# A decoder layer on one core: the two ends of SBUF swapped

## The chip, the cores and the metric

The kernel runs on one core of a Trainium2 chip. A run's time is the device time of that core in microseconds (us); before the change it is 2342.14 us, the median of three runs (2342.01 to 2342.49). Durations inside the kernel are read from one profiled execution.

## What is computed

One layer of a decoder for 256 tokens of width 2048, in float32: a SwiGLU block, a mixer of four branches, a second SwiGLU block, each followed by a residual and a layer norm.

```python
h <- LN(alpha*h + 0.5*SwiGLU_1(h))          # [256, 2048] @ [2048, 11264], then [256, 5632] @ [5632, 2048]
h <- LN(alpha*h + HybridMixer(h))           # projection, 4 causal mixers, 4 gates, 4 branch products, w_out
h <- LN(alpha*h + 0.5*SwiGLU_2(h))

def swiglu(h, w_gu, w_down):
    gate, up = jnp.split(h @ w_gu, 2, axis=-1)
    return (jax.nn.silu(gate) * up) @ w_down

# the end of the mixer: outs are the results of differential attention, GLA, MLA and SSD
merged = gates[:, :, 0] * (outs[0] @ w_branch[0])
for i in range(1, 4):
    merged = merged + gates[:, :, i] * (outs[i] @ w_branch[i])
return merged @ w_out
```

## The kernel before

**Products.** Every large product is token-major. The transposed activation (128 x 128) is the stationary operand, a weight tile (128 x 512) the moving one. A float32 product is made of three float32r ones: each operand is split exactly into a high and a low part, and `mm3` (lines 130 to 133) accumulates high x high (L131), high activation x low weight (L132) and low activation x high weight (L133). There are 9,510 such products with 512 moving columns, 192 with 300 (the narrow blocks `pm` of the input projection) and 66 with 256 (in the MLA mixer). All other products, transposes against `ident` among them, are plain float32 ones of at most 512 columns.

**The way of a weight.** `load_split` loads a group of 1 MB by DMA (SyncE's queue) into one of three buffers `raw`; `split` makes of each half of it, a chunk of 1024 columns, a tile `hi` (ScalarE, L99) and a tile `lo` (VectorE, L100); TensorE reads `hi` and `lo` as moving operands. `split` takes its tiles from two pools in turn:

```python
if self.hl2 is not None and k % 10 >= 4:
    p, b = self.hl2, 6
else:
    p, b = self.hl, 4
```

So of ten chunks the first four go to the pool `hl` and the next six to `hl2`, as long as `hl2` is open: through the first SwiGLU and the first three blocks of the projection (as `hla`), and from the output projection `wo` to the end (as `hlb`). In between, from the rest of the projection through the gates `gt` and the branch products `br`, all weights use `hl` alone, and the space of `hl2` is the mixers'.

**Order.** Each engine takes its instructions in the order in which the program writes them. The mixers' steps are put between groups of the streamed products by hand (`tick`, `MIX_STEPS`), TensorE's queue is one row of products from start to end.

**Places in SBUF.** A pool is opened at one end of SBUF, `side="left"` (low addresses, the default) or `side="right"` (high addresses), and lies against the pools opened before it at that end. A partition has 224 KB; the low end begins after 16.125 KB that are taken, the high end 32 bytes below 224 KB. All sizes in the pools of TensorE's operands at issue are whole multiples of 512 bytes or more, so what a pool starts at, counted in 64 bytes, decides for all of its tiles. The addresses in the built program (KB of a partition; the last column is the remainder of the byte address by 64):

| what | before | by 64 | after | by 64 |
|---|---|---|---|---|
| `xp`: activations, high and low part (stationary) | 18.75 to 50.75 | 0 | 16.125 to 48.125 | 0 |
| `raw`: loaded weights | 50.75 to 74.75 | 0 | 197.34 to 221.34 | 32 |
| `hl`: `hi`, then `lo` (moving) | 74.75 to 106.75 | 0 | 48.125 to 80.125 | 0 |
| `hl2`: `hi`, then `lo` (moving) | 175.97 to 223.97 | 32 | 80.125 to 128.125 | 0 |
| `oh`, `ol`: branch outputs, split (stationary in `br`) | 186.22 to 194.22 | 32 | 80.125 to 88.125 | 0 |
| `cqh`, `cql`, `ckh`, `ckl`: MLA's inner operands | 175.5 to 183.5 | 0 | 88.125 to 96.125 | 0 |
| `ident`: identity for transposes (moving) | 16.125 | 0 | 221.34 | 32 |
| `ya`: rows of the first SwiGLU (stationary in transposes) | 106.75 to 122.75 | 0 | 180.97 to 196.97 | 32 |
| `mg`: merged branches (stationary in transposes) | 158.22 to 174.22 | 32 | 129.88 to 145.88 | 0 |
| `bg`: gate biases (DMA target) | 174.22 to 178.22 | 32 | 117.88 to 121.88 | 0 |

Before, `xp` and `hl` start at multiples of 256 bytes; after, all rows with remainder 0 start at odd multiples of 128.

The functions that the change touches, with the profile's line numbers:

Of the kernel before, what the change touches and what calls it, by code (L numbers as in the profile page):

```python
"""Macaron decoder layer (SwiGLU, hybrid differential / GLA / MLA / SSD mixer, SwiGLU; post-norm).

Activations are token-major: the transposed activation is the stationary operand and each weight is
streamed once from DRAM as the moving operand. float32 products are made of float32r ones: both
operands are split exactly into two parts of 12 significant bits, and the three products that reach
float32's accuracy are accumulated in PSUM.
"""
# [9 lines left out]
F32R = mybir.dt.float32r  # L17
# [18 lines left out]
# columns of the array of constants  # L36
C_ID, C_MLE, C_MGT, C_CM, C_CUM, C_SUF, C_GM, C_IND, C_INV = 0, 128, 256, 384, 640, 768, 896, 1024, 1026
C_END = 1026 + 40
# columns of the array of parameters that are broadcast over the partitions
R_LAM, R_SUB, R_GN, R_SN, R_D, R_DTB, R_AL, R_GB, R_QN, R_KN = 0, 256, 384, 512, 1024, 1032, 1040, 1048, 1304, 1688  # L40
R_END = 1816
# blocks of the input projection
# [3 lines left out]
# steps of the mixers that go between two groups of a streamed product  # L46
MIX_STEPS = 3
# after how many runs of products a norm's parts are transposed, by token tile and part
WAIT = ((3, 4, 5, 6), (4, 5, 6, 7))
# products on zeros that bring TensorE's clock up  # L50
# [3 lines left out]
def two_pi_parts(scale, bits, n):  # L54
    """2*pi*scale as a sum of n floats: the first n-1 with so many significant bits."""
# [15 lines left out]
class Layer:  # L71
# [9 lines left out]
    def pool(self, name, side="left", bufs=1, **kw):  # L81
        return self.tc.tile_pool(name=name, bufs=bufs, side=side, reuse_waits="tile", **kw)

# [1 line left out]

    def split(self, src, n, name, step=None):
        """Exact two-part split of an f32 source into float32r tiles."""
# [15 lines left out]
    def load_split(self, w, name, fine=False):  # L103
        """One weight group [128, nk, n] -> list of (hi, lo) per k tile."""
# [30 lines left out]
    def gemm(self, name, ws, x, evac, lag=0, tail=0, pre=None, parts=None, ahead=None):  # L135
        """Token-major product: ws are weight groups [128, nk, n]; x(g, k, t) gives the stationary
        tiles; evac(t, psum) takes the result of token tile t. The second token tile follows the first
        by `lag` groups at the start, and by `tail` groups at the end. parts: groups that are loaded
        already; ahead(t): called before token tile 0 is evacuated and after token tile 1 is."""
# [38 lines left out]
    def loader(self, name, ws):  # L178
        """ahead() for the block before the one that is named: its weights are loaded and split
        before the norm in between takes the engines."""  # L180
        parts = {}

        def ahead(t):
            for g in (range(2), range(2, 3))[t]:
                parts[g] = self.load_split(ws[g], f"{name}_{g}", fine=t)

        return parts, ahead

# [30 lines left out]
    def transpose_split(self, src, name):  # L219
        """[128 tokens, 512] -> [128 of a feature tile, (4 feature tiles, 128 tokens)] in a bank."""  # L220
# [11 lines left out]
    def rstd(self, pool, ms, n, eps, name, scale=None):  # L232
        """(ms + eps) ** -0.5 for [128, n]."""
# [15 lines left out]
    def layer_norm(self, name, pool, y, stats, t, xs=None, store=None):  # L249
        """Post-norm of token tile t (in place in y); then its transposed parts, or its store."""  # L250
# [5 lines left out]
        # the first parts of the first token tile are waited for: VectorE; the others are shared out  # L256
# [12 lines left out]
        for nb in range(4):  # L269
# [6 lines left out]
            if xs is not None:  # L276
                # not before they can be ready: after so many runs of products
# [86 lines left out]
    def residual(self, y, stats, t, nb, ps):  # L364
        """y = 2 alpha h + what was accumulated, and its statistics."""
# [93 lines left out]
    def to_banks(self, pool, tag, blocks, name, bufs=3, eng=0):  # L459
        """Transposes of up to four [128, 128] blocks into one bank; copied to SBUF."""  # L460
# [12 lines left out]
    def o_room(self):  # L473
        """Lets the branch products take an earlier mixer's output first."""
        while self.o_live > 4:
            yield "full"

    def head_norm(self, pool, o, r, g, t, name):
        """o[:, h, :] * r[:, h] * g, per head of 128."""
# [18 lines left out]

    def mla(self, m):
        nc, gp = self.nc, self.gen  # L500
        with self.pool("mla", side="right") as w:
# [37 lines left out]
            # rope of the key  # L539
            cm, sm = self.cos[:, :, 8:40], self.sin[:, :, 8:40]  # L540
            yield from self.rope(w, kv[:, :, 128:160], kv[:, :, 160:192], cm, sm, [P, T, 32], "rk")
            # for even and odd heads: in one half of the rows, zeros in the other
# [6 lines left out]
            # up-projections: heads' parts without rotation come out transposed  # L549
# [127 lines left out]

    def diff(self, blk):
        nc, gp = self.nc, self.gen
        with self.pool("diff", side="right") as w:  # L680
# [7 lines left out]
            # -(lambda) = (e2 - lam_init) - e1  # L688
# [24 lines left out]
            for t in range(T):  # L713
# [5 lines left out]
                for h0 in range(0, 4, nm):  # L719
                    # the maps of a head in different rows of the array and in different banks  # L720
# [52 lines left out]

    def gla(self, blk, sm):
        nc, gp = self.nc, self.gen
        row = self.row
        with self.pool("gla", side="right") as w:
            qk, v, rr = blk[B_GQK], blk[B_GV], blk[B_GR]
            with self.pool("glaa", side="right") as wa:
# [24 lines left out]
                # sums within a chunk: up to each token, and after it  # L804
# [16 lines left out]
                # decay of the state over each chunk, per channel  # L821
# [23 lines left out]
            # states that enter chunks 1, 2, 3  # L845
# [25 lines left out]
            with self.pool("glab", side="right") as wb:  # L871
                # silu(r), twice
# [656 lines left out]
```

## Time and profile before

| | |
|---|---|
| median of three runs | 2342.14 us |
| span of the profiled execution | 2340.0 us |
| TensorE, products | 2316.7 us, 99% of the span, 10,433 instructions |
| TensorE, loads of stationary operands (beside products) | 1888.4 us, 81% |
| VectorE | 1334.5 us, 57% |
| ScalarE | 1091.1 us, 47% |
| GpSimd | 106.0 us, 5% |
| DMA | 446 MB, 191 GB/s, 55.3% of 16 engines' time |

The span runs from the first to the last instruction of the profiled execution; the median of the timed runs is 2.1 us more. Products are pipelined: one begins some 0.23 us after the one before it and is shown as 0.39 us long, so that a busy share of 99% says that TensorE hardly waits, not how fast its products follow each other. That is read from their starts, or from a count in a stretch that holds products of one kind alone.

### The profile page before, as it was taken

Reading aid. Unit: us, or ns where it says so; the run is one execution under the profiler, and the core shown is the slowest. Engines: PE = TensorE matmul, PEld = TensorE weight load, DVE = VectorE, ACT = ScalarE, POOL = GpSimd, SP = SyncE. Lnnn points to the kernel's source line nnn. Section 1 sums busy time; section 2 is a strip of 40 time slices with the busy share of each in tenths; the row PEclk is TensorE's granted clock in tenths of the full one; section 3 lists DMA queues with packets and bytes.
Section 4 is the critical chain, followed back from the end, with each engine's and each line's share of the span. In section 5 each row is a group of like instructions: output and inputs, shape, how many; then the busy total and the mean of one; then the engine's idle time right before and its main releaser. Section 6 shows DMA issues by size and latency. Waiting matters only on the chain.

```text
span 2340.0 us, 26513 instructions
## 1 busy us (share of the span) xinstructions
PE 2316.7 (99%) x10433; PEld 1888.4 (81%) x10433; DVE 1334.5 (57%) x1523; ACT 1091.1 (47%) x1400; POOL 106.0 (5%) x107
## 2 busy tenths in 40 slices
PE   9999999999999999999999999999999999999998
PEld 7888888888887988787788888887888888888886
DVE  6544444457676457646655555756444444457674
ACT  5444444455554445545444444534444444455552
POOL 0000000000001100100001011112000000000001
PEclk9999999999999999999999999999999999999999
DMA  8655555555564555454455557645555555555562
GB/s 320 221 182 192 183 181 193 184 182 195 186 228 162 176 196 171 137 191 172 167 189 201 199 198 267 233 160 191 187 182 192 183 182 193 183 183 195 185 228 72
DMA packets 73165, 446.05 MB, mean 191 GB/s; under 512 B 8513, under 2 KB 8913, under 8 KB 22865
## 3 DMA queue, kind: packets, MB, share of 16 engines
q1 hardware_dynamic: 73040, 444.37, 55.3%
q8 instruction: 81, 1.33, 0.2%
q14 instruction: 44, 0.35, 0.0%
HBM read 440.15 MB, written 4.19 MB: 190 GB/s over the span
## 4 chain that ended last, share of the span: by engine, by line
PE 97%; DVE 1%; POOL 0%; ACT 0%; issue 0%; DMA 0%; POOLq 0%; SPq 0%; DVEq 0%; ACTq 0%
PE f_gu_ps L132 14%; PE f_gu_ps L133 14%; PE f_gu_ps L131 14%; PE f_dn_ps L131 7%; PE f_dn_ps L132 7%; PE f_dn_ps L133 7%; PE gt_ps L131 5%; PE gt_ps L133 5%; PE gt_ps L132 5%; PE pj_ps L133 3%; PE pj_ps L132 3%; PE pj_ps L131 3%; PE br_ps L131 1%; PE br_ps L133 1%; PE br_ps L132 1%; PE wo_ps L131 1%
## 5 line engine op out<-in xcount | busy, mean ns | idle before, releaser
L100 DVE TENSOR_TENSOR f_gu_lo<-f_gu_raw,f_gu_hi 128x1024 fp32r<-128x1024 f32 (+1 forms) x362 | 434.6, 1207 | 435.0 <-ACT f_gu_hi L99 425.2
L99 ACT CAST f_gu_hi<-f_gu_raw 128x1024 fp32r<-128x1024 f32 (+1 forms) x362 | 370.1, 1027 | 451.5 <-PE f_gu_ps L133 415.3
L131 PE MATMUL f_gu_ps<-f_gu_hi,n_x_h 128*128 128x512 f32 x704 | 281.5, 400 | 0.4 <-ACT n_x_h L229 0.4
L131 PE MATMUL f_gu_ps<-f_gu_hi,x_h 128*128 128x512 f32 x704 | 280.9, 399 | 0.6 <-ACT f_gu_hi L99 0.6
L133 PE MATMUL f_gu_ps<-f_gu_hi,n_x_l 128*128 128x512 f32 x704 | 277.4, 394 | 3.3 <-DVE n_x_l L230 3.3
L132 PE MATMUL f_gu_ps<-f_gu_lo,x_h 128*128 128x512 f32 x704 | 277.0, 394 | 0.5 <-DVE f_gu_lo L100 0.5
L132 PE MATMUL f_gu_ps<-f_gu_lo,n_x_h 128*128 128x512 f32 x704 | 277.4, 394 | 0.0
L131 PE MATMUL f_dn_ps<-f_dn_hi,f_a_h 128*128 128x512 f32 x704 | 277.2, 394 | 0.0
L132 PE MATMUL f_dn_ps<-f_dn_lo,f_a_h 128*128 128x512 f32 x704 | 276.8, 393 | 0.0
L133 PE MATMUL f_dn_ps<-f_dn_hi,f_a_l 128*128 128x512 f32 x704 | 276.6, 393 | 0.0
L133 PE MATMUL f_gu_ps<-f_gu_hi,x_l 128*128 128x512 f32 x704 | 276.4, 393 | 0.0
L100 DVE TENSOR_TENSOR f_dn_lo<-f_dn_raw,f_dn_hi 128x1024 fp32r<-128x1024 f32 x176 | 215.0, 1222 | 35.2 <-ACT f_dn_hi L99 34.7
L100 DVE TENSOR_TENSOR gt_lo<-gt_raw,gt_hi 128x1024 fp32r<-128x1024 f32 x128 | 156.8, 1228 | 134.6 <-ACT gt_hi L99 130.1
L336 ACT CAST f_a_h<-f_act 128x512 fp32r<-128x512 f32 x176 | 108.8, 618 | 209.8 <-PE f_dn_ps L132 200.0
L99 ACT CAST gt_hi<-gt_raw 128x1024 fp32r<-128x1024 f32 x128 | 134.6, 1053 | 149.9 <-PE gt_ps L133 107.4
L131 PE MATMUL gt_ps<-gt_hi,n_x_h 128*128 128x512 f32 x512 | 200.0, 391 | 0.0
L132 PE MATMUL gt_ps<-gt_lo,n_x_h 128*128 128x512 f32 x512 | 199.4, 389 | 0.0
L133 PE MATMUL gt_ps<-gt_hi,n_x_l 128*128 128x512 f32 x512 | 199.4, 389 | 0.0
L337 DVE TENSOR_TENSOR f_a_l<-f_act,f_a_h 128x512 fp32r<-128x512 f32 x176 | 121.2, 689 | 120.0 <-ACT f_a_h L336 120.0
L99 ACT CAST f_dn_hi<-f_dn_raw 128x1024 fp32r<-128x1024 f32 x176 | 184.5, 1048 | 9.8 <-PE f_gu_ps L133 9.8
L133 PEld LDWEIGHTS f_gu_ps<-f_gu_hi,n_x_l 128*128 128x128 f32 x704 | 132.7, 188 | 34.2 <-DVE n_x_l L230 3.8
L132 PEld LDWEIGHTS f_gu_ps<-f_gu_lo,x_h 128*128 128x128 f32 x704 | 132.5, 188 | 30.1 <-DVE f_gu_lo L100 1.8
(366 smaller groups left out, 3390.2 us busy)
## 6 DMA issues: line engine op xcount, KB each, us to landing
f_gu_raw<-in_wgu SPq DMA_DIRECT2D x172, 1024.0 KB, 4.8
f_dn_raw<-in_wdn SPq DMA_DIRECT2D x88, 1024.0 KB, 4.9
gt_raw<-in_wg SPq DMA_DIRECT2D x64, 1024.0 KB, 4.9
pj_raw<-in_wp SPq DMA_DIRECT2D x36, 1024.0 KB, 4.8
br_raw<-in_wb SPq DMA_DIRECT2D x16, 1024.0 KB, 4.8
wo_raw<-in_wo SPq DMA_DIRECT2D x16, 1024.0 KB, 4.8
pm_raw<-in_wm SPq DMA_DIRECT2D x8, 600.0 KB, 4.3
f_gu_raw<-in_wgu SPq DMA_DIRECT2D x16, 256.0 KB, 5.5
```

The costliest lines, as they stand in the source:

```text
L99: nc.scalar.copy(hi[:, c], src[:, c])
L100: nc.vector.tensor_tensor(lo[:, c], src[:, c], hi[:, c].bitcast(F32), op=ALU.subtract)
L131: nc.tensor.matmul(ps, xh, wh, start=start, stop=False)
L132: nc.tensor.matmul(ps, xh, wl, start=False, stop=False)
L133: nc.tensor.matmul(ps, xl, wh, start=False, stop=stop)
L336: nc.scalar.copy(hi, src)
L337: nc.vector.tensor_tensor(lo, src, hi.bitcast(F32), op=ALU.subtract)
```

## The change

`pool()` opens pools at the high end unless told otherwise, and the pools that held a side explicitly change it. With that, `xp`, `hl`, `hl2` and the mixers' own pools (`mla`, `diff`, `gla`, `ssd` and their inner ones) lie at the low end; constants and `ident` (`cp`), `raw`, the rows of activations, the mixer's constants and outputs at the high end. `oh` and `ol` leave the pool of the gates for a new one, `mxl`, which is opened at the low end when `hla` is closed. Comments and docstrings are removed as well. The diff without those:

```diff
-    def pool(self, name, side="left", bufs=1, **kw):
+    def pool(self, name, side="right", bufs=1, **kw):
...
-        with self.pool("mla", side="right") as w:
+        with self.pool("mla", side="left") as w:
...   (diff, gla, glaa, glab, ssd, ssda, ssdb in the same way)
             self.hl2 = None
             hl_pool.close()
+            ml = st.enter_context(self.pool("mxl", side="left"))
...
-                    hi = mp.tile([P, 512], F32R, tag="oh", bufs=2, name=f"oh{i}_{t}")
-                    lo = mp.tile([P, 512], F32R, tag="ol", bufs=2, name=f"ol{i}_{t}")
+                    hi = ml.tile([P, 512], F32R, tag="oh", bufs=2, name=f"oh{i}_{t}")
+                    lo = ml.tile([P, 512], F32R, tag="ol", bufs=2, name=f"ol{i}_{t}")
...
-        self.xp = ent(self.pool("xp"))
+        self.xp = ent(self.pool("xp", side="left"))
         self.rawp = ent(self.pool("rawp"))
-        self.hl = ent(self.pool("hl"))
+        self.hl = ent(self.pool("hl", side="left"))
...
-            self.hl2 = st.enter_context(self.pool(name, side="right"))
+            self.hl2 = st.enter_context(self.pool(name, side="left"))
```

No instruction is added, removed or moved: on every engine the built program has the same instructions in the same order. What differs beside addresses is which semaphores an instruction waits for where a tile takes over another tile's place: in 8 instructions of VectorE, 31 of ScalarE, 16 of GpSimd and 15 DMA issues of SyncE, and in none of TensorE. The tables of addresses above are the change.

## Rows read from the trace of the kernel before

**Rows 1.** The page, parts 1 and 2: busy time; the granted clock in 40 slices.

```profile
PE 2316.7 (99%) x10433; PEld 1888.4 (81%) x10433; DVE 1334.5 (57%) x1523; ACT 1091.1 (47%) x1400; POOL 106.0 (5%) x107
PEclk9999999999999999999999999999999999999999
```

**Rows 2.** The page, part 4: the chain that ended last, shares by engine.

```profile
PE 97%; DVE 1%; POOL 0%; ACT 0%; issue 0%; DMA 0%; POOLq 0%; SPq 0%; DVEq 0%; ACTq 0%
```

**Rows 3.** Waits of TensorE: line, releaser, us in total, times, longest; the longest three.

```profile
PE f_gu_ps L133 <- DVE n_x_l L230: 3.3, 1, 3.3
PE pj_ps L133 <- DVE n_x_l L230: 3.3, 1, 3.3
PE diff_q L704 <- DVE pj L442: 1.6, 1, 1.6
```

**Rows 4.** Stretches of TensorE: from:to, us, PE busy (count), clock, DMA share, GB/s.

```profile
1264.73:1308.02 43.29, 43.29 (x192) 1.00 0.57 200
1253.54:1264.50 10.96, 10.96 (x48) 1.00 0.60 198
510.47:745.76 235.29, 235.29 (x1022) 1.00 0.56 193
780.30:806.75 26.45, 26.45 (x192) 1.00 0.68 227
4.90:32.60 27.70, 26.61 (x108) 1.00 0.88 320
```

**Rows 5.** TensorE in order of time, in `f_gu`: start us, us, line, operands.

```profile
299.69 0.39 PE L131 MATMUL f_gu_ps<-f_gu_hi,x_h 128*128 128x512 f32 x1
...
301.05 0.40 PE L131 MATMUL f_gu_ps<-f_gu_hi,x_h 128*128 128x512 f32 x1
301.28 0.40 PE L132 MATMUL f_gu_ps<-f_gu_lo,x_h 128*128 128x512 f32 x1
...
303.15 0.40 PE L131 MATMUL f_gu_ps<-f_gu_hi,x_h 128*128 128x512 f32 x1
```

**Rows 6.** The same view, in the MLA mixer: `ckh`, `ckl` stationary.

```profile
849.74 0.39 PE L131 MATMUL mla_v<-ukv_hi,ckh 128*128 128x512 f32 x1
849.96 0.39 PE L132 MATMUL mla_v<-ukv_lo,ckh 128*128 128x512 f32 x1
850.19 0.39 PE L133 MATMUL mla_v<-ukv_hi,ckl 128*128 128x512 f32 x1
850.42 0.39 PE L131 MATMUL pj_ps<-pj_hi,n_x_h 128*128 128x512 f32 x1
```

**Rows 7.** The same view, 256 columns: second and last of 54 in a row.

```profile
830.19 0.28 PE L132 MATMUL mla_q<-cql,uq_hi 128*128 128x256 f32 x1
...
836.43 0.28 PE L133 MATMUL mla_qr<-uq_hi,cql 128*128 128x256 f32 x1
```

**Rows 8.** Groups by line: transposes against `ident`; count, busy us, mean ns, idle before.

```profile
L224 PE MATMUL n_tp<-ident,ya 128*128 128x128 f32 x32 | 4.8, 272 | 0.0
L224 PE MATMUL mT_tp<-ident,mg 128*128 128x128 f32 x32 | 4.1, 272 | 0.0
```

**Rows 9.** The page, parts 5, 3 and 6: splits; DMA queue; DMA issues, KB, us to landing.

```profile
L100 DVE TENSOR_TENSOR f_gu_lo<-f_gu_raw,f_gu_hi 128x1024 fp32r<-128x1024 f32 (+1 forms) x362 | 434.6, 1207 | 435.0 <-ACT f_gu_hi L99 425.2
L100 DVE TENSOR_TENSOR gt_lo<-gt_raw,gt_hi 128x1024 fp32r<-128x1024 f32 x128 | 156.8, 1228 | 134.6 <-ACT gt_hi L99 130.1
q1 hardware_dynamic: 73040, 444.37, 55.3%
f_gu_raw<-in_wgu SPq DMA_DIRECT2D x172, 1024.0 KB, 4.8
bg<-in_b_gate SPq DMA_DIRECT2D x16, 256.0 KB, 3.4
f_gb<-in_ln_g SPq DMA_DIRECT2D x8, 256.0 KB, 3.4
```

More of the change, by code (lines that the diff above doesn't have):

```diff
@@ L679, in diff @@
         nc, gp = self.nc, self.gen
-        with self.pool("diff", side="right") as w:
+        with self.pool("diff", side="left") as w:
             row = self.row
@@ L776, in gla @@
         row = self.row
-        with self.pool("gla", side="right") as w:
+        with self.pool("gla", side="left") as w:
             qk, v, rr = blk[B_GQK], blk[B_GV], blk[B_GR]
-            with self.pool("glaa", side="right") as wa:
+            with self.pool("glaa", side="left") as wa:
                 w2 = wa.tile([16, 256], F32, name="gla_w2")
@@ L870, in gla @@
                 yield
-            with self.pool("glab", side="right") as wb:
+            with self.pool("glab", side="left") as wb:
                 sr = wb.tile([P, T, 512], F32, name="gla_sr")
@@ L950, in ssd @@
         row = self.row
-        with self.pool("ssd", side="right") as w:
+        with self.pool("ssd", side="left") as w:
             x = w.tile([P, T, 8], F32, name="dt_x")
@@ L982, in ssd @@
             yield
-            with self.pool("ssda", side="right") as wa:
+            with self.pool("ssda", side="left") as wa:
                 xc = [(wa if j < 2 else w).tile([P, 2, 256], F32, name=f"ssd_xc{j}") for j in range(4)]
@@ L1023, in ssd @@
                 yield
-            with self.pool("ssdb", side="right") as wb:
+            with self.pool("ssdb", side="left") as wb:
                 BT, CT = xc[2], xc[3]
```

## The prediction

> **What bounds the kernel now.** I read the page's busy times first, then the chain, then TensorE's waits, then stretches of TensorE with one kind of product each, and last single products in order of time. TensorE is busy for 99% of the span, at a granted clock of nine tenths or more in all forty slices, which is the upper of its two levels, 2.4 GHz [rows 1]; 97% of the chain that ended last is TensorE's own work [rows 2]; and the longest waits in its list are 3.3, 3.3 and 1.6 us [rows 3]. So there is almost nothing to wait for. What can be won is how fast one product follows another, and this the busy share hides, since a product is shown as 0.39 us long while the next one begins after 0.23 us.
>
> So I count starts. In the gates `gt` 192 products with 512 columns take 43.29 us from the first start to the last, which is 191 steps of 226.6 ns. In the branch products `br`, whose instruction is the same, 48 take 10.96 us: 47 steps of 233.2 ns. In `f_dn` some 1,020 steps take 235.29 us: 230.7 ns. [rows 4] (A count may hold a product or two that run in from ahead.) Weights come from `hl` alone in `gt` and `br`. In `f_dn` they come from `hl` for four chunks of ten and from `hl2` for six, and 0.4 x 226.6 + 0.6 x 233.2 = 230.6, which is what is seen if products on `hl2` take the step of `br`. The single products show that it is so: in one block of `f_gu` six products on an `hl` chunk take 301.05 - 299.69 = 1.36 us, 226.7 ns each, and the nine that follow, on `hl2` chunks with the same kind of stationary operand, take 303.15 - 301.05 = 2.10 us, 233.3 ns each [rows 5]. The step changes at the product where the chunk's pool changes. At 2.4 GHz, 226.7 ns are 544 cycles and 233.3 ns are 560: the slow step is 16 cycles longer.
>
> What slow products have in common is one operand at the high end: `hl2` tiles (moving) or `oh`, `ol` (stationary, in `br`). These lie both high, above 175 KB, and at a remainder of 32 bytes by 64, because the high end begins 32 bytes below 224 KB. The trace has a few products that separate the two. The last three products of `mla_v` have stationary operands at 182 and 183 KB, high but at remainder 0: they start at 849.74, 849.96, 850.19 and the next at 850.42, three steps of 226.7 ns [rows 6]. With 256 columns, 36 of 54 products have moving operands at 175.5 to 183.5 KB, remainder 0, the other 18 stationary ones there: 52 steps in 6.24 us, 120.0 ns [rows 7], which is 256 cycles and the same 32 on top as the fast step. So the condition is more likely the remainder than the height. The 300-column products in `pm` step at 26.45 us / 191 = 138.5 ns [rows 4], 300 cycles and 32, on both pools alike; they start 1200 bytes apart inside a chunk, at several remainders, and do not separate the two.
>
> **The change part by part.**
>
> *Moving operands.* 4,056 products with 512 columns read a weight from `hl2` in the built program: 2,520 in `f_gu`, 1,248 in `f_dn`, 216 in `wo`, 72 in `pj`. After the change `hl2` lies low and at remainder 0. Each should step at 226.7 instead of 233.3 ns: 4,056 x 6.67 ns = 27.0 us.
>
> *Stationary operands.* 384 products of `br` get `oh` and `ol` at the low end, remainder 0: 384 x 6.67 ns = 2.6 us. Together 29.6 us, all of it on TensorE, which is the chain.
>
> *Where the gain is not on the path.* From 4.9 to 32.6 us, 108 products take 27.70 us, 259 ns a step, since the first weights are still coming (320 GB/s) [rows 4]; some 59 of them read `hl2`, so up to 59 x 6.67 = 0.4 us is not won. I take off the 0.4.
>
> *`ident` moves to the high end at remainder 32.* Some 400 plain float32 transposes with 128 columns read it as moving operand. The trace has none with a moving operand at that remainder. The nearest rows are those where the stationary side is at it (`mg`, remainder 32) and where it isn't (`ya`): both 272 ns [rows 8]. From this I take 0. The upper end is the step of the float32r products for each, 400 x 6.67 = 2.7 us; a gain is excluded, since `ident` lay at remainder 0 already.
>
> *`raw` moves to remainder 32.* VectorE's split takes 1,207 ns in `f_gu`, where six of ten destinations are at remainder 32, and 1,228 ns in `gt`, where none is [rows 9]; no row has the source there. VectorE at 57% and ScalarE at 47% [rows 1] have room for a third more, so I take 0 with no end that reaches the path. For the DMA, 256 KB to `bg` (remainder 32) land in 3.4 us and 256 KB to `f_gb` (remainder 0) in 3.4 us [rows 9]: 0. A group of weights is needed every 24 x 226.7 ns = 5.4 us and lands 4.8 us after its issue with three buffers, while the queue is busy for 55.3% of 16 engines' time [rows 9]; it would have to become 1.8 times as slow before TensorE waits.
>
> A rule speaks against this move. The Trainium skill, DMA: Bandwidth & Descriptors, section "How a descriptor splits into AXI transactions", says that a descriptor which does not start on 256 bytes spends an extra transaction; `raw` starts on such a boundary before and not after. By that page, a row of 8 KB would be 33 transactions instead of 32, an estimated 3% more, so 55.3% would become about 57%, and the sum would stay the same.
>
> *Waits.* No wait of TensorE changes in the program. The changed ones on other engines stand where pools change hands, ahead of the mixers and of `hlb`; those engines run ahead of TensorE by up to ten chunks there. 0, with 1 us as the upper end, the size of the third of the longest waits now [rows 3].
>
> Sum: the span goes from 2340.0 to 2340.0 - 29.6 + 0.4 = 2310.8 us. The median of the runs is 2.1 us above the span, and I carry that over: 2342.1 - 29.2 = **2312.9 us**, 1.2% faster. The unknowns reach from -0.4 (the start gains too) to +2.7 + 1.0, so 2312.5 to 2316.6 by themselves; for the steps, which are read to about 0.2 ns over 9,500 products, I add 2 us on either side.
>
> **The rivals.**
>
> *The edge is lower than all slow rows.* If height decides, the edge lies anywhere between 107 KB (fast) and 176 KB (slow). At 112 KB, the middle of the partition, the four upper `lo` tiles of `hl2` (112.1 to 128.1 KB) would stay slow: 900 products of L132, 6.0 us. Time 2318.9. [rows 6] speak against height at all.
>
> *Nothing changes.* The slow step would come from the turn in the ring, or from what else runs while `hl2` is read, not from the place: 2342.1. Against it: `br` has the slow step with weights from `hl`, and it begins and ends with the operand [rows 4]. For it: only that the trace never shows a low operand at remainder 32. By a statement of the Trainium skill (SBUF — State Buffer, "Door 1", on cachelines) SBUF has lines of 16 bytes, and an access pays where it crosses to a new line; by that, addresses at remainder 32 are as good as those at 0, and this rival's time would follow. The trace disagrees where `br` takes 233.2 ns and `gt` 226.6.
>
> *Slower: the grid is 256 bytes.* All fast 512-column products of before have operands at multiples of 256. After the change every operand is at an odd multiple of 128. If a product needs 256, all 9,510 take the slow step, and the 5,064 fast ones of now lose 5,064 x 6.67 = 33.8 us: 2375.9. It decides as soon as an operand off 256 costs what one off 64 does. Against it: 256 more columns cost 226.7 - 120.0 = 106.7 ns, which is a column a cycle, so in the 16 cycles of the slow step 64 bytes of a moving operand pass, not 256; for it: no row has a float32r operand at an odd multiple of 128.
>
> *Slower by the DMA.* If a `raw` at remainder 32 doubles the queue's time, 55.3% of 2340 us become 2,588 us and the queue is the bound; it decides from 1.8 times on. The equal landings of `bg` and `f_gb` [rows 9] speak against it.
>
> **How the numbers follow.** The forecast 0.80 (remainder or height, both give it), the edge at 112 KB 0.05, a gain of another size between 5 and 25 us 0.03, nothing 0.05, the 256-byte grid 0.06, the DMA 0.01. What a measurement can tell from no change is about 0.2%, 4.7 us. Faster: 0.80 + 0.05 + 0.03 = 0.88; same: 0.05; slower: 0.07. The forecast's own range, 2310.5 to 2318.6, nearly holds the case of the 112 KB edge, which takes it to 2319 and to 0.85 less the forecast's own tails.
>
> **What the profile after would show.** `f_dn` steps at 226.7 to 227 ns, so its 235.3 us become 231.5; `br` steps as `gt` does; in `f_gu` there is no change of step between chunks. With the edge at 112 KB, L132 products alone step slowly for two chunks of five. With the 256-byte grid, `gt` steps at 233.3 too. If transposes pay for `ident`, their pairs in `f_gu` begin farther apart. The prediction is wrong if `gt` changes its step at all, or if waits of TensorE on `hi` or `lo` appear inside the SwiGLU blocks.

## The result

The kernel after takes 2317.06 us (median of four runs, 2316.57 to 2317.88), the kernel before 2342.07 us in the runs beside them: a ratio of 0.9891, 95% interval 0.9877 to 0.9905. That is 1.1% less, clear of the noise and inside the range; the forecast was 2312.9 us, 4.2 us too low. The profiled execution has a span of 2314.4 us, 25.6 us less than before, where 29.2 us were predicted.

Of the page of the kernel after, the lines that answer to [rows 1] and [rows 9] (busy us, share of the span, instructions; the clock in tenths; the queue's packets, MB and share; the splits of VectorE):

```profile
PE 2290.9 (99%) x10433; PEld 1888.6 (82%) x10433; DVE 1335.0 (58%) x1523; ACT 1089.4 (47%) x1400; POOL 106.2 (5%) x107
PEclk9999999999999999999999999999999999999999
q1 hardware_dynamic: 73040, 444.37, 55.9%
L100 DVE TENSOR_TENSOR f_gu_lo<-f_gu_raw,f_gu_hi 128x1024 fp32r<-128x1024 f32 (+1 forms) x362 | 434.9, 1208 | 423.1 <-ACT f_gu_hi L99 403.6
L100 DVE TENSOR_TENSOR gt_lo<-gt_raw,gt_hi 128x1024 fp32r<-128x1024 f32 x128 | 156.9, 1229 | 133.3 <-ACT gt_hi L99 128.7
```

TensorE has the same instructions and 25.8 us less to be busy with; its clock is as high as before. The other engines and the queue do what they did, though `raw` now lies at another remainder: the splits take 1208 and 1229 ns, before 1207 and 1228.

The longest waits of TensorE after (us in total, times, longest), as in [rows 3]:

```profile
PE f_gu_ps L133 <- DVE n_x_l L230: 3.4, 1, 3.4
PE pj_ps L133 <- DVE n_x_l L230: 3.4, 1, 3.4
PE diff_q L704 <- DVE pj L442: 1.6, 1, 1.6
```

So no wait took the place of what was saved. The stretches of [rows 4] in the kernel after: `f_dn`, `gt`, `br` and the start (from:to, us, PE busy and count, clock, DMA share, GB/s). Here and below a stretch runs from the start of its first product to that of its last, 1,019 steps in `f_dn`, 191 in `gt`, 47 in `br`; the count of the row also takes in products that run in from ahead.

```profile
503.46:734.57 231.11, 231.11 (x1023) 1.00 0.59 197
1252.68:1295.98 43.30, 43.30 (x193) 1.00 0.58 203
1241.80:1252.46 10.66, 10.66 (x49) 1.00 0.59 194
5.92:32.10 26.18, 26.18 (x108) 1.00 0.91 332
```

A step of `f_dn` takes 226.8 ns (before, 235.29 us by the same 1,019 steps: 230.9), one of `br` 226.8 (before 233.2), one of `gt` 226.7 as before. In `f_gu` the step no longer changes where the chunk changes its pool. These are the same three products as in [rows 5], the second where `hl2` begins (start us, us, line, operands):

```profile
295.69 0.39 PE L131 MATMUL f_gu_ps<-f_gu_hi,x_h 128*128 128x512 f32 x1
...
297.05 0.39 PE L131 MATMUL f_gu_ps<-f_gu_hi,x_h 128*128 128x512 f32 x1
...
299.09 0.39 PE L131 MATMUL f_gu_ps<-f_gu_hi,x_h 128*128 128x512 f32 x1
```

Six products in 1.36 us, then nine in 2.04 us: 226.7 ns both, where the nine took 2.10 us before.

**Where the 25.6 us come from.** I took every product with 512 columns whose moving operand was one of the two that the prediction counted (a weight in `hl2`, or any weight against `oh`, `ol`), and compared its step, start to start, in the two traces. "Near others" are those among the first nine products after transposes or another short product.

| products | number | ns less, each | us less |
|---|---|---|---|
| clear of others | 3,649 | 6.6 | 24.1 |
| near others | 658 | 2.0 | 1.3 |
| last of a row, and those of the first stretch | 132 | 3.3 | 0.4 |
| all else on TensorE, the start and the waits among it | | | -0.2 |

By block these products gave 14.0 us in `f_gu`, 8.2 in `f_dn`, 1.4 in `wo`, 0.2 in `pj` and 2.0 in `br`.

### The profile page after: what moved, and what is told of

Same layout as the page of the kernel before. It is cut to its first block, busy times and chain, and to the rows that moved or that the text cites. A ratio compares the mean times of both kernels' runs of the same rounds, so it can differ in the third digit from the quotient of the medians.

```text
span 2314.4 us, 26513 instructions
## 1 busy us (share of the span) xinstructions
PE 2290.9 (99%) x10433; PEld 1888.6 (82%) x10433; DVE 1335.0 (58%) x1523; ACT 1089.4 (47%) x1400; POOL 106.2 (5%) x107
## 3 DMA queue, kind: packets, MB, share of 16 engines
q1 hardware_dynamic: 73040, 444.37, 55.9%
## 4 chain that ended last, share of the span: by engine, by line
PE 97%; DVE 1%; POOL 0%; ACT 0%; issue 0%; DMA 0%; POOLq 0%; DVEq 0%; SPq 0%; ACTq 0%
PE f_gu_ps L133 14%; PE f_gu_ps L131 14%; PE f_gu_ps L132 14%; PE f_dn_ps L131 7%; PE f_dn_ps L132 7%; PE f_dn_ps L133 7%; PE gt_ps L131 5%; PE gt_ps L133 5%; PE gt_ps L132 5%; PE pj_ps L133 3%; PE pj_ps L132 3%; PE pj_ps L131 3%; PE br_ps L131 1%; PE br_ps L133 1%; PE br_ps L132 1%; PE wo_ps L133 1%
## 5 line engine op out<-in xcount | busy, mean ns | idle before, releaser
L100 DVE TENSOR_TENSOR f_gu_lo<-f_gu_raw,f_gu_hi 128x1024 fp32r<-128x1024 f32 (+1 forms) x362 | 434.9, 1208 | 423.1 <-ACT f_gu_hi L99 403.6
L131 PE MATMUL f_gu_ps<-f_gu_hi,n_x_h 128*128 128x512 f32 x704 | 279.2, 397 | 0.5 <-ACT n_x_h L229 0.5
L131 PE MATMUL f_gu_ps<-f_gu_hi,x_h 128*128 128x512 f32 x704 | 278.6, 396 | 0.7 <-ACT f_gu_hi L99 0.7
L133 PE MATMUL f_gu_ps<-f_gu_hi,n_x_l 128*128 128x512 f32 x704 | 275.4, 391 | 3.4 <-DVE n_x_l L230 3.4
L133 PE MATMUL f_gu_ps<-f_gu_hi,x_l 128*128 128x512 f32 x704 | 275.0, 391 | 0.0
L132 PE MATMUL f_gu_ps<-f_gu_lo,n_x_h 128*128 128x512 f32 x704 | 274.9, 390 | 0.0
L132 PE MATMUL f_gu_ps<-f_gu_lo,x_h 128*128 128x512 f32 x704 | 274.7, 390 | 0.0
L131 PE MATMUL f_dn_ps<-f_dn_hi,f_a_h 128*128 128x512 f32 x704 | 274.3, 390 | 0.0
L133 PE MATMUL f_dn_ps<-f_dn_hi,f_a_l 128*128 128x512 f32 x704 | 273.9, 389 | 0.0
L132 PE MATMUL f_dn_ps<-f_dn_lo,f_a_h 128*128 128x512 f32 x704 | 273.9, 389 | 0.0
L100 DVE TENSOR_TENSOR gt_lo<-gt_raw,gt_hi 128x1024 fp32r<-128x1024 f32 x128 | 156.9, 1229 | 133.3 <-ACT gt_hi L99 128.7
L131 PE MATMUL gt_ps<-gt_hi,n_x_h 128*128 128x512 f32 x512 | 200.0, 391 | 0.0
L132 PE MATMUL gt_ps<-gt_lo,n_x_h 128*128 128x512 f32 x512 | 199.4, 389 | 0.0
L133 PE MATMUL gt_ps<-gt_hi,n_x_l 128*128 128x512 f32 x512 | 199.4, 389 | 0.0
L133 PEld LDWEIGHTS f_gu_ps<-f_gu_hi,n_x_l 128*128 128x128 f32 x704 | 132.5, 188 | 32.1 <-DVE n_x_l L230 3.8
L131 PEld LDWEIGHTS f_gu_ps<-f_gu_hi,x_h 128*128 128x128 f32 x704 | 132.6, 188 | 28.1 <-ACT f_gu_hi L99 2.0
```

The source lines that it names most:

```text
L100: nc.vector.tensor_tensor(lo[:, c], src[:, c], hi[:, c].bitcast(F32), op=ALU.subtract)
L131: nc.tensor.matmul(ps, xh, wh, start=start, stop=False)
L132: nc.tensor.matmul(ps, xh, wl, start=False, stop=False)
L133: nc.tensor.matmul(ps, xl, wh, start=False, stop=stop)
```

## The experiments

The prediction left the cause open between two readings, the place's height and an operand's own remainder by 64 bytes. The trace of before could not separate them, and both were wrong. What stands at the end is called theory C' in the expectations: **it counts whether the moving operand of a product and the stationary operand that is loaded meanwhile, the next product's, start at the same remainder by 256 bytes.** In the kernel before, activations and `hl` are at 0 by 256, `hl2`, `oh` and `ol` at 224; after, all are at 128.

### The high end moved by 32 bytes, in the kernel before

```diff
 (kernel before, ahead of the constants)
+        ent(self.pool("padr", side="right")).tile([P, 8], F32, name="padr")
```

> The kernel before, with 32 unused bytes at the very top of SBUF. hl2 stays at the high end (176 to 224 KB) and comes to remainder 0 by 64; oh and ol stay at remainder 32. Theory A (the start of an operand on a grid of 64 bytes decides): the products on hl2 step at 226.7 ns, those of br still at 233.3; time 2317 us, since the trace after shows 25.0 us for the products that read hl2. Theory B (height decides): nothing moves, 2342 us, f_dn steps at 230.7 ns. If the grid is 128 bytes, hl2 (64 by 128) stays slow as in B.

2344.02 us, ratio to before 1.0007 (0.9998 to 1.0017). The stretch of `f_dn`:

```profile
510.77:746.05 235.28, 235.28 (x1023) 1.00 0.57 193
```

It is 235.29 us in [rows 4]. `hl2` is now at remainder 0 by 64, and nothing changed: a multiple of 64 is not enough for the fast step. (By 256 the weights are at 192, the activations at 0.)

### The low `hl2` moved by 32 bytes, in the kernel after

```diff
+            st.enter_context(self.pool(name + "p", side="left")).tile([P, 8], F32, name=name + "p")
             self.hl2 = st.enter_context(self.pool(name, side="left"))
```

> The kernel after, with 32 unused bytes ahead of hl2: hl2 stays at the low end (80 to 128 KB) but at remainder 32 by 64; all else as after. Theory A: hl2 products step at 233.3 ns again, f_dn at 230.7; 25 us lost, 2342 us. Theory B: as after, 2317 us, f_dn at 226.8 ns.

2342.21 us, ratio 0.9999 (0.9989 to 1.0009): with 32 bytes the whole gain is gone. `f_dn`, then `br`:

```profile
510.00:745.43 235.43, 235.43 (x1022) 1.00 0.57 193
1364.88:1375.54 10.66, 10.66 (x49) 1.00 0.60 195
```

`hl2` is low, and its products step at 233.3 ns. Height is refuted. `br`, whose weights come from `hl`, stays at 226.8 ns.

### All of the low end moved by 32 bytes, in the kernel after

```diff
+        ent(self.pool("padl", side="left")).tile([P, 8], F32, name="padl")
         self.xp = ent(self.pool("xp", side="left"))
```

> The kernel after, with 32 unused bytes ahead of all of TensorE's large operands: stationary and moving ones at the low end, all at remainder 32 by 64. Theory A, one step of 16 cycles for either operand or both: gt, br, f_dn all step at 233.3 ns; some 9,510 products lose 6.67 ns less what lies near transposes, 58 to 63 us, 2375 to 2380 us. Theory A with a step for each operand: 240 ns, 2435 us. Theory B: as after, 2317 us.

2318.19 us, ratio 0.9898 (0.9883 to 0.9913), `f_dn`:

```profile
503.70:734.80 231.10, 231.10 (x1023) 1.00 0.59 197
```

Every operand is at remainder 32 by 64 (160 by 256), and every product is fast. With the run before this refutes the reading of the prediction, in which remainder 32 was slow by itself. What the two runs differ in is whether weights and activations lie alike.

### Several remainders for `hl2`, in the kernel after

```diff
-        hi = p.tile([P, 1024], F32R, tag="whi", bufs=b, name=f"{name}_hi")
-        lo = p.tile([P, 1024], F32R, tag="wlo", bufs=b, name=f"{name}_lo")
+        o = (0, 1, 4, 8, 12, 15)[k % 10 - 4] if p is self.hl2 else 0
+        w = 1040 if p is self.hl2 else 1024
+        hi = p.tile([P, w], F32R, tag="whi", bufs=b, name=f"{name}_hi")[:, o : o + 1024]
+        lo = p.tile([P, w], F32R, tag="wlo", bufs=b, name=f"{name}_lo")[:, o : o + 1024]
```

> The kernel after, with each of the six tiles of hi and of lo in hl2 read and written from an offset of its own, 0, 4, 16, 32, 48 and 60 bytes, in tiles of 4160 bytes. Theory A on a grid of 64: offset 0 steps at 226.7 ns, all others at 233.3, the same whatever the offset; f_dn steps at 230.0 (half of the products). If the step grows with the offset, the five differ from each other. If a grid of 16 or 32 bytes is meant, 16, 32 and 48 or 32 alone are fast. Theory B: all at 226.7.

2338.73 us in one run; `f_dn`:

```profile
510.61:745.50 234.89, 234.89 (x1023) 1.00 0.57 194
```

That is 230.5 ns a step. Over all products with 512 columns that are clear of others, sorted by the difference of the two starts by 256, every difference that occurs (16, 48, 60, 68, 96, 112, ... 252) has a mean step of 229 to 237 ns, 0 has 227.3. A difference of 128, which a rule by 64 or by 128 bytes would let pass, takes 234.0.

### The low parts of the activations moved by 32 bytes, in the kernel after

```diff
-            self.xp.tile([P, 512], F32R, tag="xl", bufs=8, name=f"{name}_l"),
+            self.xp.tile([P, 576], F32R, tag="xl", bufs=8, name=f"{name}_l")[:, 8:520],
```

> The kernel after, with the low parts of the activations (stationary in L133) 32 bytes off; high parts and all weights stay at the remainder that they share by 256. Theory C (a product is slow when its moving operand and the stationary operand that is loaded while it runs, that of the next product, start at different remainders): L132, ahead of L133, steps at 233.3 ns; L131 and L133 stay at 226.7; f_dn 228.9 on the mean, about 2337 us. Theory D (a product's own two operands must agree): the same mean, but it is L133 that steps at 233.3 and L132 stays at 226.7.

2373.04 us in one run. `f_dn`, `gt`, `br`:

```profile
515.39:753.24 237.85, 237.85 (x1023) 1.00 0.56 191
1394.08:1438.64 44.56, 44.56 (x192) 1.00 0.56 199
1383.19:1393.86 10.67, 10.67 (x49) 1.00 0.58 186
```

One stationary operand of three is off, and all of `f_dn` and `gt` step at 233.4 and 233.3 ns on the mean, as if all were; `br`, whose low part `ol` was not moved, stays at 227.0. Neither theory had said this. By line, over `f_dn` and `gt`: the product after which the moved operand is needed (L132) takes 239.2 ns, the one that uses it (L133) 228.4, the one where neither holds (L131) 232.3. So the cost falls on the product during which the odd operand is loaded, and part of it on the next one. That the load and the product before it go side by side shows in the trace of before, where the load for L133 (PEld) begins with the product of L132:

```profile
299.91 0.39 PE L132 MATMUL f_gu_ps<-f_gu_lo,x_h 128*128 128x512 f32 x1
299.92 0.19 PEld L133 LDWEIGHTS f_gu_ps<-f_gu_hi,x_l 128*128 128x128 f32 x1
```

Why one in three costs as much as three in three, 20 ns in every three products, stays open.

### Every difference in steps of 16 bytes, chunk by chunk

```diff
+        o = (0, 4, 8, 12, 16, 20, 24, 28, 32, 36)[k % 10]
+        hi = p.tile([P, 1088], F32R, tag="whi", bufs=b, name=f"{name}_hi")[:, o : o + 1024]
```

(and `lo` alike; the second kernel has 40, 44, 48, 52, 56, 60, 64, 1, 2, 6 in the place of these words of four bytes)

> The kernel after, where the ten chunks of a turn start 0, 16, 32, 48, 64, 80, 96, 112, 128 and 144 bytes off the remainder by 256 of the stationary operands, hi and lo alike. Theory C with a period of 256: 226.7 ns for 0 alone and 229 to 236 ns for the others; mean of f_dn near 232.5. If the period is 128, 128 is as fast as 0. If equal remainders are not the best place but only a good one, another difference is under 226.7.

> As the scan before it, at differences of 160, 176, 192, 208, 224, 240, 256, 4, 8 and 24 bytes. Theory C with a period of 256: 256 is as fast as 0, 226.7 ns; 192 and 224 at 233.3 as seen before. 4, 8 and 24 tell whether a difference inside 16 or 32 bytes costs as much as a larger one: if lines of 16 bytes matter, 4 and 8 are at 226.7.

2364.07 and 2373.82 us in one run each; `f_dn` takes 236.06 and 237.41 us.

All differences took 229 to 237 ns. But the chunks with the difference 0 took 231.1 too, and those with 256 took 230.7, so these runs can't tell one from another: a chunk gives only six products in a row before the difference changes, and in the run with several remainders the step needed ten to come to 226.7 ns after a change to 0. The next run gives it the room.

### One difference for a whole block of weights

The kernel after, with 24 blocks of `gt` and `f_dn` off by one amount each and all others by 0:

```diff
+OFF = {'gt2_0': 4, 'gt2_1': 8, 'gt2_2': 16, 'gt2_3': 48, 'gt3_0': 64, 'gt3_1': 80, 'gt3_2': 96, 'gt3_3': 112, 'gt0_0': 128, 'gt0_1': 144, 'gt0_2': 160, 'gt0_3': 176, 'gt1_0': 208, 'gt1_1': 240, 'gt1_2': 256, 'gt1_3': 12, 'f0_dn0': 64, 'f0_dn1': 128, 'f0_dn2': 16, 'f0_dn3': 240, 'f2_dn0': 8, 'f2_dn1': 96, 'f2_dn2': 176, 'f2_dn3': 256}
...
+        o = OFF.get(name.rsplit("_", 2)[0], 0) // 4
+        hi = p.tile([P, 1088], F32R, tag="whi", bufs=b, name=f"{name}_hi")[:, o : o + 1024]
+        lo = p.tile([P, 1088], F32R, tag="wlo", bufs=b, name=f"{name}_lo")[:, o : o + 1024]
```

> The kernel after; in 24 blocks of weights both parts of every weight lie some bytes off (4 to 256, one amount per block), everything else at offset 0. Here whole blocks of 72 to 240 products have one and the same difference between the moving operand and the stationary operand loaded meanwhile, so that the step can settle. Theory C' (equal start by 256 bytes gives the 544-cycle step, everything else a longer one): blocks at 256 step at 226.7 ns, all others at 229 to 240 ns, 233.3 on the mean; the 24 blocks hold some 3,800 products, so about 2317 + 3,700 x 6.7 ns = 2342 us. Rival G (the step depends on the amount, and some differences are shorter than 544 cycles because the two streams keep out of each other's way): at least one block steps below 226 ns. Rival H (only multiples of 64 by a finer grid matter, and what was seen at 64 or 128 was the change from chunk to chunk): blocks at 64, 128 and 256 step at 226.7.

2341.77 us in one run. Five blocks, off by 64, 128, 4, 112 and 256 bytes (240, 264, 96, 96 and 263 steps):

```profile
503.83:558.86 55.03, 55.03 (x244) 1.00 0.55 189
558.86:620.20 61.34, 61.34 (x266) 1.00 0.55 189
1017.90:1040.68 22.78, 22.78 (x97) 1.00 0.52 191
1230.47:1252.64 22.17, 22.17 (x97) 1.00 0.58 204
2268.07:2327.77 59.70, 59.70 (x265) 1.00 0.30 105
```

They step at 229.3, 232.3, 237.3, 230.9 and 227.0 ns. The mean steps by difference over all blocks, in ns, without the products near others:

| bytes off | 0, 256 | 4 | 8 | 12 | 16 | 48 | 64 | 80 | 96 | 112 | 128 | 144 | 160 | 176 | 208 | 240 |
|---|---|---|---|---|---|---|---|---|---|---|---|---|---|---|---|---|
| step | 226.8 | 237.3 | 232.7 | 229.0 | 231.7 | 233.3 | 229.0 | 231.0 | 233.4 | 231.0 | 232.6 | 233.3 | 234.2 | 232.7 | 234.7 | 235.8 |

256 is as good as 0, no other amount is, and none is better: rivals G and H fall. Between them the cost goes from 2.3 ns (12 and 64 bytes) to 10.6 ns (4 bytes) without an order that I can read.

### The identity of the transposes put at the same remainder

The kernel after; after two transposes in `f_gu` the products step more slowly for a while, and this asks whether addresses are the cause there too.

```diff
+        ent(self.pool("padr", side="right")).tile([P, 56], F32, name="padr")
```

> The kernel after with 224 bytes left free at the high end, so that the identity of the transposes (and the rows of the SwiGLU that they take) start at 128 by 256 bytes, as the activations and weights do. After two transposes, the next six products of the kernel after take up to 88 ns more for the first and 1.5 to 10 ns more for the others, until the step is 226.7 ns again. Theory C' carried over to transposes: this comes from the identity's start differing from the weights'; with it equal the five later products step at 226.7 ns, some 88 pairs x 23 ns = 2.0 us less: 2315.0 us. Rival: the step must settle anew after any change of the kind of product, whatever the addresses: 2317.1 us, the same six steps.

2315.74 us (2314.98 to 2316.16), ratio 0.9883 (0.9867 to 0.9900), an interval that overlaps that of the kernel after. The times don't tell the two apart; the steps do. Each block of `f_gu` has two pairs of transposes, one for each half of the tokens. Behind the first pair the steps are alike in both kernels: six products in 1.47 us, the first of them 0.31, then 226.7 ns. Behind the second the first six products take 1.47 us too, but the four that follow differ. The seventh and the eleventh product there in the kernel after:

```profile
282.06 0.40 PE L131 MATMUL f_gu_ps<-f_gu_hi,x_h 128*128 128x512 f32 x1
...
282.99 0.39 PE L132 MATMUL f_gu_ps<-f_gu_lo,x_h 128*128 128x512 f32 x1
```

and with the identity moved:

```profile
282.71 0.39 PE L131 MATMUL f_gu_ps<-f_gu_hi,x_h 128*128 128x512 f32 x1
...
283.62 0.39 PE L132 MATMUL f_gu_ps<-f_gu_lo,x_h 128*128 128x512 f32 x1
```

The four steps take 0.93 and 0.91 us: ten products are slow in the kernel after, six here. In nanoseconds of the trace that is 21 ns behind each of 43 second pairs, 0.9 us; none is won behind the first ones. The two profiled executions have the same span all the same, since this one waits longer for its first weights (2.0 us on `f_gu_hi` in its list of waits, 0.7 in the kernel after).

So neither expectation holds. Products two to six stay slow with equal starts, so theory C' doesn't carry over; but the place of the identity, or of the SwiGLU's rows that moved with it, has a part in how long the step takes to settle. Equality isn't needed for the shorter of the two: in the last kernel below the identity lies 128 bytes from the weights by 256, and the first eleven steps take 2.606 us behind either pair, as they do here. What decides stays open.

### Activations and weights 32 bytes apart, all of them low

```diff
+        ent(self.pool("padl", side="left")).tile([P, 8], F32, name="padl")
         self.xp = ent(self.pool("xp", side="left"))
+        ent(self.pool("padm", side="left")).tile([P, 8], F32, name="padm")
         self.hl = ent(self.pool("hl", side="left"))
```

(on the kernel after; `rawp`, opened between them, lies at the other end)

> The kernel after with 32 bytes left free below the activations and 32 more behind them: weights at 192, activations at 160 by 256 bytes, all at the low end; the branch outputs, which are stationary in the branch products, stay at the same remainder as the weights. Theory C': every product on an activation pays, gt, f_gu, f_dn step at 233 ns on the mean, while the 384 branch products and the few products on the MLA mixer's operands stay at 226.7 ns: 2317.1 + 9,126 x 6.67 ns = 2378 us at most. Theory A (an operand's own remainder by 64, with weights at 0): gt and f_gu slow as well, since activations are at 32; but the branch products and gt could not differ if the place of the weights decided: then all at 226.7 and 2317 us, or all slow.

2371.42 us in one run. `f_dn`, `gt`, `br`:

```profile
515.08:752.93 237.85, 237.85 (x1023) 1.00 0.55 191
1394.00:1438.56 44.56, 44.56 (x192) 1.00 0.56 197
1383.11:1393.76 10.65, 10.65 (x48) 1.00 0.58 193
```

`gt` and `br` stand beside each other and read weights from the same tiles of `hl`. `gt`, on activations at 160, steps at 233.3 ns; `br`, on `oh` and `ol` at 192 like the weights, at 226.6. No property of the weights' place alone can do that.

Where the two meet, it also shows which stationary operand counts, a product's own or the next one's. The last product of `br` starts alike with its own operand (`ol`, at 192), while the next product's (`n_x_h`) is at 160:

```profile
1393.76 0.40 PE L133 MATMUL br_ps<-br_hi,ol 128*128 128x512 f32 x1
1394.00 0.39 PE L131 MATMUL gt_ps<-gt_hi,n_x_h 128*128 128x512 f32 x1
```

All ten products of `br` that stand ahead of one of `gt` take 235 ns, the other products of `br` that are clear of short ones 226.8 on the mean; in the kernel after, where all starts are alike, the same ten take 227.2. The other way round, the seven products of `gt` ahead of one of `br` step at 229.6 ns here, though their own operand is off. In the kernel before, where theirs is not off and the next one's is, they take 233.7.

### The kernel before, nothing swapped, starts made equal

```diff
 (kernel before, ahead of the constants)
+        ent(self.pool("padr", side="right")).tile([P, 56], F32, name="padr")
```

> The kernel before, nothing swapped, with 224 bytes left free at the high end: hl2 stays at 176 to 224 KB, but its tiles start at 0 by 256 bytes as the activations do (before: 224 by 256). Theory C' (only the equality of moving and next stationary operand counts): f_dn steps at 226.8 ns, the pure stretches of f_gu at 228.3 ns, and the time falls by what f_gu, f_dn, wo and pj gained through the swap, 14.7 + 8.6 + 1.5 + 0.2 = 25.0 us, to 2317.1 us; the branch products, whose stationary operands stay at 224, stay at 233 ns. Rival (a low place is needed as well): 2342.1 us as before and f_dn at 230.7 ns.

```diff
 (and in the mixer, in the second kernel)
             mp = st.enter_context(self.pool("mxm"))
+            mp.tile([P, 8], F32, name="padm")
```

> As the kernel with 224 bytes free at the high end, and 32 bytes more ahead of the mixer's pool, so that the branch outputs oh and ol start at 0 by 256 bytes too, at 186 KB. Theory C': the branch products step at 226.7 ns in addition, 2.0 us less than the kernel without these 32 bytes: 2315.1 us, the time of the kernel after within a few us, with two unused pieces in place of the swap. Rival (a low place is needed for the stationary operand): branch products stay at 233 ns and the time equals that of the kernel without these 32 bytes.

With 224 bytes left free: 2318.61 us, ratio 0.9895 (0.9880 to 0.9910). `f_dn`, `gt`, `br`:

```profile
503.15:734.24 231.09, 231.09 (x1023) 1.00 0.59 197
1364.71:1408.00 43.29, 43.29 (x192) 1.00 0.57 200
1353.52:1364.48 10.96, 10.96 (x48) 1.00 0.63 199
```

With 32 more ahead of `oh` and `ol`: 2315.92 us (2314.70 to 2316.07), ratio 0.9883 (0.9866 to 0.9899), `br`:

```profile
1351.97:1362.63 10.66, 10.66 (x49) 1.00 0.63 201
```

The first brings all but `br`, at 176 to 224 KB; the second brings `br` as well, with its operands at 186 KB. Two unused pieces of 224 and 32 bytes do what the swap does. The second is 1.1 us below the median of the kernel after, but the intervals overlap: the two are not told apart, and no run can be told apart from these as faster.

## Why the prediction was right, and which of its steps were not

The forecast came true with the wrong cause: its count of starts was sound, its choice of a cause was lucky.

**What bounds the kernel, and the step of 16 cycles:** right. TensorE stays busy for 99%, the waits stay, and what was won is the step, 6.6 ns on each of 3,649 products against 6.67 predicted. The sign and most of the size rest on this count of starts, not on a cause.

**The cause:** wrong. The step that failed is "the condition is more likely the remainder than the height", with the remainder taken for each operand by itself and by 64. Height plays no part (32 bytes off at the low end: 2342.21 us; equal starts at the high end: 2318.61 us), nor does an operand's own remainder (all at 32: 2318.19 us). It is the equality of the two starts by 256. The rows used for the choice fit this as well: `ckh` in [rows 6] and [rows 7] is at 0 by 256, like the weights beside it, and `hl2` at 224 is not. And [rows 7] could not have told a fast place from a slow one: with 256 columns starts that are 32 bytes apart cost nothing (117.2 ns against 119.8 with equal ones, below). I had asked what the slow products have in common, and not what their two operands have in common. The forecast came out because the swap happens to make all starts equal, 128 by 256. The same reasoning would have promised some 2315 us (26.6 less, `br` unchanged) for the 32 bytes at the high end of the kernel before, which took 2344.02.

**Where `oh` and `ol` get their remainder:** a slip. They were said to be off because the high end begins 32 bytes below 224 KB. That holds for `hl2`; `oh` and `ol` lay on the stack of the low end, and owed their 224 to the odd sizes below them. With the high end moved by 224 bytes they stayed slow (10.96 us), as the run above shows.

**The slower rival, the grid of 256 bytes:** rightly given little, for a wrong reason. By it all products would be slow after; `gt` takes 43.30 us as before. There is a period of 256 bytes, but it belongs to the difference of two starts.

**The sum of 29.6 us:** too large by 3.1 us in one term. 658 of the 4,440 products stand among the first nine after transposes or short products, and these gained 2.0 instead of 6.67 ns. Their step is not settled at either level. The same pair of transposes on an `hl2` chunk, before:

```profile
281.34 0.38 PE L313 MATMUL f_at<-ident,f_sg 128*128 128x128 f32 x2
281.48 0.48 PE L131 MATMUL f_gu_ps<-f_gu_hi,x_h 128*128 128x512 f32 x1
...
282.95 0.40 PE L131 MATMUL f_gu_ps<-f_gu_hi,x_h 128*128 128x512 f32 x1
```

and after:

```profile
277.48 0.38 PE L313 MATMUL f_at<-ident,f_sg 128*128 128x128 f32 x2
277.62 0.48 PE L131 MATMUL f_gu_ps<-f_gu_hi,x_h 128*128 128x512 f32 x1
...
279.09 0.39 PE L131 MATMUL f_gu_ps<-f_gu_hi,x_h 128*128 128x512 f32 x1
...
279.77 0.39 PE L131 MATMUL f_gu_ps<-f_gu_hi,x_h 128*128 128x512 f32 x1
```

The six products behind the pair take 1.47 us both times; only from the seventh on does the kernel after have its 226.7 ns (0.68 us for three). `f_gu`, with 88 such pairs, therefore gained 14.0 us in place of 16.8, `br`, with the mixers' short products between its rows, 2.0 in place of 2.6; `f_dn` and `wo`, which have almost none, gave 8.2 and 1.4, where 8.3 and 1.4 were predicted.

**The start:** 0.4 us were written off and 0.3 of them came. The first product of `f_gu` begins 1.02 us later (5.92 against 4.90 us), but 108 steps on, at 32.5 us, the kernel after is 0.5 us ahead. In the other runs this first start lies between 4.9 and 5.7 us, on either layout, so that it belongs to the run, not to the change.

**The edits costed at nothing:** `raw`, the DMA and the waits, all right. The splits and waits are shown above; the queue's share went from 55.3% to 55.9% of a span that is 1.1% shorter, which is the same time, so that the 3% more that were estimated for a `raw` off 256 bytes did not come.

**`ident` at remainder 32:** not quite nothing. The second pair of a block is followed by ten slow products in the kernel after. With `ident` where it lay before, six are slow on `hl` chunks of the kernel before, and the shorter settling holds for all chunks in the last kernel above. As the run with the identity moved shows, that is 0.9 us, inside the upper end of 2.7, and part of what the sum was too large by.

**The median:** it lies 2.7 us above the profiled span, where 2.1 were carried over. With the 3.6 us that the span is longer than predicted (2314.4 to 2310.8) this makes the 4.2 us. The profiled execution was the fastest of the four timed ones (2316.57 us), which is where most of the 0.6 us between the two comes from.

## What to carry to other kernels

On an engine that is busy for 99% of the time, measure the step from start to start for each kind of product and each pool that its operands come from: a busy share hides 3% there. Where products of one shape step differently, compare the start addresses of the two operands with each other, by 256 bytes, before looking at where they lie; padding a pool to make them equal (here 224 and 32 bytes) does what a new layout does. A gain per product counts only for products that stand clear of short ones, here from the seventh to the eleventh on.

## What the runs showed of the hardware

- With float32r operands, 512 columns and a new stationary operand for each product, TensorE steps at 226.7 ns (544 cycles at 2.4 GHz) when the moving operand and the next product's stationary one start at the same remainder by 256 bytes, and at 229 to 237 ns, in most layouts 233.3 (560 cycles), when they don't. That it is the next product's, and not the product's own, is shown by L132 and L133 above and by the products between `br` and `gt`. That the two reads get in each other's way is argued from this and not shown by itself.
- The Trainium skill, TensorE: Matmul & The Clock Gate, section "Step-by-step: what each phase is for", says that TensorE has two independent read ports, and that loading the next stationary operand takes no read bandwidth from the running product. In the runs here the two are not independent in time: 32 bytes between their starts cost 233.3 against 226.7 ns. Whether read bandwidth is the reason, no run shows.
- With 300 columns (`pm`) no such cost is seen: 191 steps take 26.45 us before ([rows 4]), where one product in six has equal starts, and 26.51 us after, where half have.
- With 256 columns it is the other way round, if little: 53 steps of the MLA mixer's products take 6.35 us in the kernel after, with equal starts, and 6.21 us with 224 bytes free in the kernel before, where its operands are 32 bytes apart from the weights: 119.8 and 117.2 ns.

```profile
818.85:825.20 6.35, 6.35 (x55) 1.00 0.56 201
```

```profile
818.70:824.91 6.21, 6.21 (x54) 1.00 0.55 199
```

- The step has a memory. With equal starts it takes six or ten products to come to 226.7 ns after a pair of transposes in the kernel after. After a change from `hl2` to `hl`, unequal to equal, it takes five in the kernel before (231.5, 230.5, 227.3, 229.3 and 228.4 ns on the mean of 47 changes); after one from equal to unequal the step is 233.3 ns on the mean at once.
